# Score products of the first attention: two 128-row passes and four 32-row products side by side, two units at a time

## The chip, the cores and the metric

One core of a Trainium2 chip runs the whole kernel. The metric is the device time of one execution in microseconds. Five engines work side by side, each through its own queue in order: TensorE (PE, with its weight loads PEld), VectorE (DVE), ScalarE (ACT), GpSimd (POOL) and SyncE (SP), which issues the DMAs. They wait for each other through semaphores. TensorE writes to PSUM, here eight banks of 128 x 512 float32. VectorE and ScalarE read it from there.

## The reference

An encoder of two layers over 1024 positions of width 1024. Layer 0 is multi-head latent attention with 16 heads, layer 1 is differential attention. The change lies in layer 0:

```python
sc = (jnp.einsum('bqhd,bkhd->bhqk', qn, k_nope)
      + jnp.einsum('bqhd,bkd->bhqk', qr, k_rope))
p = jax.nn.softmax(sc.astype(jnp.float32), axis=-1)
return jnp.einsum('bhqk,bkhd->bqhd', p.astype(v.dtype), v)
```

`qn` and `k_nope` have 64 elements for each head, `qr` and `k_rope` have 32, and `k_rope` is the same for all heads. Everything is float32.

## The kernel before

Products keep float32's precision by splitting each operand in a high part, rounded to the type fp32r, and a low part, the rest. A product of two operands is then three matmuls: high by high, high by low, low by high.

**Layout.** For each head the keys lie in `Kh` (high) and `Kl` (low), 96 rows by 1024 columns: rows 0 to 63 are `k_nope`, rows 64 to 95 the rotated `k_rope`. The queries of a head and half lie in one page `Q` of 96 rows: `Q[:, 0]` high, `Q[:, 1]` low, 512 columns each. Three buffers of `Kh` and `Kl` go round over the heads; the rope rows of two of them are copied by DMA before the stage. The rope rows of the queries were computed earlier, went to DRAM (`RD`), and come back by two DMAs of 64 KB for each head and half (L820).

**A unit** is one head and one tile of 128 queries; there are 128 units, numbered head by head, eight to a head. `Unit0.scores` makes 128 x 1024 scores by six matmuls of 96 rows and 512 columns (L868 to L870) into a PSUM tile `S` of two banks. `maximum` (L874, DVE) takes the row maximum. `softmax` makes the exponentials with their row sums (L879, ACT), the reciprocal of the sums (L880, DVE) and the scaled page `p` (L881, POOL). Then `transposes` turns `p` into two PSUM tiles `T` by eight 128 x 128 transposes (L845), and `split` takes each `T` out as a high part (ACT, in the helper `hi`, L97) and a low part (DVE, L853). The low part reads `T` and the high part. Two units make a `Chunk`; `pv0` multiplies its 256 columns with the values by 16 matmuls (L905), and `out0` takes the result out: a copy (L913, ACT), an addition (L914, DVE), a product with the gate (L915, POOL).

PSUM holds two `S` tiles, two `T` tiles and two `A` tiles, eight banks in all.

**The order** is written out by hand for all engines: each engine runs its instructions in the order in which the loop emits them. The loop goes over steps `u` from -2 to 129. Step `u` scores unit `u + 2`, finishes the softmax of unit `u + 1`, transposes and splits unit `u`, and on even steps multiplies the chunk of units `u - 2` and `u - 1`:

```python
units[u + 2].scores()                  # PE
units[u + 1].softmax()                 # ACT, DVE, POOL
ps = pv0(ch // 4, chunks[ch])          # even steps: PE
tps = chunks[u // 2].transposes(units[u])
units[u + 2].maximum()                 # DVE
chunks[u // 2].split(units[u], tps)    # ACT, DVE, twice
out0(ch // 4, ch % 4, ps)              # even steps
for fn in fill.get(u, ()): fn()
```

**Fills** are other work put at the end of chosen steps. For each later pair of heads (seven of them, 16 steps each) four odd steps hold a half of the keys or the queries: `k_half` (six matmuls of 512 columns, then two copies on ACT, two subtractions on DVE) and `q_half` (nine matmuls, two copies of 64 x 512 at L822, two subtractions at L825, and the DMAs of the rope rows). Twelve steps hold a part of the values (`v_rows`). Steps 44, 52, ... 100 make a tile of distances for the second layer on DVE (`dist_tile`, L962 and L963), with its absolute value on ACT (L1072) in the step behind. The output projection's weights are split in odd steps from 105 on. The keys and queries of the first two heads are made before the stage, while TensorE works on the gates.

All large tiles come from one pool of 49 pages of 4 KB for each partition.

In the second layer `Unit1.scores` (L1333) multiplies 64-row operands: two matmuls in turn, on rows 0 to 63 and on rows 64 to 127.

Of the kernel before, what the change touches and what calls it, by code (L numbers as in the profile page):

```python
# [21 lines left out]
NPAGES = 49  # L22
# [33 lines left out]
def body(tc, x, c, positions, ada_w, ada_b, norm_g, mla_w_in, mla_q_norm_g, mla_w_q_up,  # L56
# [4 lines left out]
    with ctx:  # L61
# [533 lines left out]
        latH, latL, Kh, Kl, lats = [], [], [], [], {}  # L595
# [39 lines left out]
        def lat_turn(hf):  # L635
# [15 lines left out]
            if hf == 0:  # L651
                Kh.append(page((QK0, D), F32R, "Kh"))
                Kl.append(page((QK0, D), F32R, "Kl"))
            hi("A", Kh[0][NOPE:QK0, sl], tp[0:ROPE, :])
            V.tensor_tensor(Kl[0][NOPE:QK0, sl], tp[0:ROPE, :], f(Kh[0][NOPE:QK0, sl]), op=ALU.subtract)
# [134 lines left out]
        Qt = {}  # L790
# [21 lines left out]
        def q_half(pr, qw, hf, psum=A_):  # L812
# [3 lines left out]
            for i in range(2):  # L816
                h = 2 * pr + i
                q = Qt[h, hf] = page((QK0, 2, 512), F32R, "Q")
                for z in range(2):
                    nc.sync.dma_start(f(q[NOPE:QK0, z]), f(RD[z, h, :, hf * 512:(hf + 1) * 512]))  # L820
                src = ps[i * 64:(i + 1) * 64, :]
                A.activation(q[0:64, 0], src, AF.Copy, scale=SC0)  # L822
            for i in range(2):
                q, src = Qt[2 * pr + i, hf], ps[i * 64:(i + 1) * 64, :]
                V.scalar_tensor_tensor(q[0:64, 1], src, SC0, f(q[0:64, 0]), op0=ALU.mult, op1=ALU.subtract)  # L825

        def k_half(pr, kw, hf, psum=A_):
# [3 lines left out]
            for i in range(2):  # L831
                b = (2 * pr + i) % 3
                src = ps[i * 64:(i + 1) * 64, :]
                hi("A", Kh[b][0:64, sl], src)
            for i in range(2):
                b = (2 * pr + i) % 3
                src = ps[i * 64:(i + 1) * 64, :]
                V.tensor_tensor(Kl[b][0:64, sl], src, f(Kh[b][0:64, sl]), op=ALU.subtract)
# [16 lines left out]
        class Unit0:  # L855
# [4 lines left out]

            def scores(self):
                q = Qt[self.h, self.qt // 4]
                b = self.h % 3
                sl = slice((self.qt % 4) * P, (self.qt % 4 + 1) * P)
                self.ps = S_()
                for n in range(2):
                    kn = slice(n * 512, (n + 1) * 512)
                    T.matmul(self.ps[:, n], q[:, 0, sl], Kh[b][:, kn], start=True, stop=False)  # L868
                    T.matmul(self.ps[:, n], q[:, 0, sl], Kl[b][:, kn], start=False, stop=False)  # L869
                    T.matmul(self.ps[:, n], q[:, 1, sl], Kh[b][:, kn], start=False, stop=True)  # L870
# [5 lines left out]
            def softmax(self):  # L876
                l = cl(1, "l", 4)
                p = self.p = page(name="p")
                A.activation(p.rearrange("p (a b) -> p a b", b=512), self.ps, AF.Exp, bias=self.m, accum_out=l)  # L879
# [735 lines left out]
```

## Time and profile before

| what | value |
|---|---|
| median of three runs | 1628.02 us (1627.78 to 1628.41) |
| the profiled execution | 1632.43 us, of it 1630.7 us from the first to the last instruction |
| busy shares of that span | PE 95%, PEld 81%, DVE 73%, ACT 51%, POOL 28% |
| first score matmul of layer 0 | 246.5 us |
| last score matmuls of layer 0 | from 748.8 us |

Times inside the profile count from its first instruction. A row of the timeline gives start, duration, engine, line, operation, output and inputs, and in brackets how long the engine had been idle and what ended that. Instructions of one kind that follow each other are one row, with their count. The duration of a matmul runs on past the start of the next one, so the pace of TensorE is read from starts, not from durations.

### The profile page before, as it was taken

Reading aid. Unit: us, or ns where it says so; the run is one execution under the profiler, and the core shown is the slowest. Engines: PE = TensorE matmul, PEld = TensorE weight load, DVE = VectorE, ACT = ScalarE, POOL = GpSimd, SP = SyncE. Lnnn points to the kernel's source line nnn. Section 1 sums busy time; section 2 is a strip of 40 time slices with the busy share of each in tenths; the row PEclk is TensorE's granted clock in tenths of the full one; section 3 lists DMA queues with packets and bytes.
Section 4 is the critical chain, followed back from the end, with each engine's and each line's share of the span. In section 5 each row is a group of like instructions: output and inputs, shape, how many; then the busy total and the mean of one; then the engine's idle time right before and its main releaser. Section 6 shows DMA issues by size and latency. Waiting matters only on the chain. (4 is left out here: it accounts for less than half of the span.)

```text
span 1630.7 us, 24823 instructions
## 1 busy us (share of the span) xinstructions
PE 1556.4 (95%) x9231; PEld 1328.9 (81%) x9231; DVE 1183.4 (73%) x2260; ACT 824.1 (51%) x1633; POOL 463.1 (28%) x436
## 2 busy tenths in 40 slices
PE   5999999999999999999999999999999999998897
PEld 4997887888888888888887888788877887776786
DVE  5476877888988888885546667777776677677764
ACT  6343126766777777784123444444543444444511
POOL 1032544444444453572352111111111011110422
PEclk8799999999999999999999999999999999999899
DMA  9007851100110111211233123423232223125122
GB/s 362 30 23 252 259 171 62 45 27 28 53 53 28 65 35 47 96 48 40 103 119 127 65 91 104 130 78 117 78 104 77 92 78 117 52 74 198 46 97 91
DMA packets 91586, 153.32 MB, mean 94 GB/s; under 512 B 5873, under 2 KB 60231, under 8 KB 91465
## 3 DMA queue, kind: packets, MB, share of 16 engines
q1 hardware_dynamic: 91464, 151.73, 28.0%
q8 instruction: 73, 1.20, 0.3%
q14 instruction: 49, 0.39, 0.1%
HBM read 126.01 MB, written 25.17 MB: 93 GB/s over the span
## 5 line engine op out<-in xcount | busy, mean ns | idle before, releaser
L853 DVE TENSOR_TENSOR ptl<-T,pth 128x512 fp32r<-128x512 f32 x384 | 246.3, 683 | 42.2 <-ACT pth L97 42.2
L97 ACT ACTIVATE pth<-T 128x512 fp32r<-128x512 f32 x384 | 207.4, 590 | 92.7 <-PE T L845 87.4
L1339 DVE CUSTOM_DVE_ANT_0 p<-S,dist 128x1024 f32<-128x1024 f32 x128 | 156.1, 1220 | 118.9 <-PE S L1333 111.0
L1347 ACT ACTIVATE p<-p,m 128x1024 f32<-128x1024 f32 x128 | 147.6, 1153 | 172.5 <-DVE m L1341 160.3
L104 POOL TENSOR_TENSOR wbl<-wblk,wbh 128x1024 fp32r<-128x1024 f32 x32 | 77.4, 2423 | 524.9 <-DVE wbh L99 326.9
L845 PE MATMUL T<-ident,p 128*128 128x128 f32 x1536 | 208.0, 278 | 7.0 <-DVE ptl L853 4.0
L845 PEld LDWEIGHTS T<-ident,p 128*128 128x128 f32 x1536 | 172.2, 141 | 44.7 <-issue 13.8
L881 POOL TENSOR_SCALAR p<-p,l 128x1024 f32<-128x1024 f32 x128 | 144.1, 1126 | 152.7 <-DVE l L880 106.7
L1199 PE MATMUL A<-hT,wbh 128*128 128x512 f32 x408 | 164.7, 404 | 1.9 <-DVE KK L1211 1.9
L1200 PE MATMUL A<-hT,wbh 128*128 128x512 f32 x408 | 160.4, 393 | 0.0
L1201 PE MATMUL A<-hT,wbl 128*128 128x512 f32 x408 | 159.9, 392 | 0.0
L874 DVE TENSOR_REDUCE m<-S 128x1 f32<-128x1024 f32 x128 | 155.9, 1218 | 2.3 <-PE S L870 0.3
L879 ACT ACTIVATE p<-S,m 128x1024 f32<-128x1024 f32 x128 | 143.1, 1118 | 14.6 <-DVE m L874 9.8
L868 PE MATMUL S<-Kh,Q 96*128 96x512 f32 x256 | 108.7, 425 | 5.3 <-ACT p L879 3.6
L1333 PE MATMUL S<-KK,QQ 64*128 64x512 f32 x768 | 109.5, 415 | 3.6 <-DVE m L1339 3.6
L869 PE MATMUL S<-Kl,Q 96*128 96x512 f32 x256 | 100.9, 394 | 0.0
L870 PE MATMUL S<-Kh,Q 96*128 96x512 f32 x256 | 100.8, 394 | 0.0
L1199 PEld LDWEIGHTS A<-hT,wbh 128*128 128x128 f32 x408 | 77.3, 189 | 17.6 <-DVE KK L1211 2.4
L1333 PEld LDWEIGHTS S<-KK,QQ 64*128 64x128 f32 x768 | 69.0, 188 | 27.2 <-issue 6.4
L915 POOL TENSOR_TENSOR og<-ot,og 64x256 f32<-64x256 f32 x64 | 54.1, 845 | 130.6 <-DVE ot L914 128.5
L1201 PEld LDWEIGHTS A<-hT,wbl 128*128 128x128 f32 x408 | 77.3, 190 | 16.8
L1200 PEld LDWEIGHTS A<-hT,wbh 128*128 128x128 f32 x408 | 77.5, 190 | 14.7
(342 smaller groups left out, 3508.0 us busy)
## 6 DMA issues: line engine op xcount, KB each, us to landing
dist<-DD SPq DMA_DIRECT2D x64, 512.0 KB, 4.0
adaw<-in_ada_w_dram SPq DMA_DIRECT2D x48, 512.0 KB, 6.6
wblk<-in_diff_w_in_dram SPq DMA_DIRECT2D x32, 512.0 KB, 5.6
qraw<-in_mla_w_q_up_dram SPq DMA_DIRECT2D x16, 288.0 KB
x<-in_x_dram SPq DMA_DIRECT2D x8, 512.0 KB, 5.7
wraw<-in_mla_w_in_dram SPq DMA_DIRECT2D x8, 512.0 KB
OGD<-gt SPq DMA_DIRECT2D x8, 512.0 KB, 6.9
Q<-RD SPq DMA_DIRECT2D x64, 64.0 KB, 2.0
```

Source lines behind the costliest of these rows:

```text
L97: A.activation(o, i, AF.Copy)
L845: T.transpose(tp[:, i * P:(i + 1) * P], p[:, kt * P:(kt + 1) * P], ident)
L853: V.tensor_tensor(ptl[n][:, :, o], src, f(pth[n][:, :, o]), op=ALU.subtract)
L874: V.tensor_reduce(self.m, self.ps, axis=AX.XY, op=ALU.max, negate=True)
L879: A.activation(p.rearrange("p (a b) -> p a b", b=512), self.ps, AF.Exp, bias=self.m, accum_out=l)
L881: G.tensor_scalar(p, p, l, 1.0, op0=ALU.mult, op1=ALU.mult)
L1199: T.matmul(ps, w[0][:, k], a, start=k == 0, stop=False)
L1200: T.matmul(ps, w[0][:, k], b, start=False, stop=False)
L1201: T.matmul(ps, w[1][:, k], a, start=False, stop=k == 7)
L1333: T.matmul(self.ps[c_][:, n], q[r, zq, sl], k[zk][r, n * 512:(n + 1) * 512], start=i == 0, stop=i == 2)
L1339: V.tensor_tensor_reduce(out=p, in0=self.ps[c_].rearrange("p a b -> p (a b)"), in1=dist[self.u], op0=ALU.subtract, op1=ALU.max, scale=1.0, ...
L1347: A.activation(p, p, AF.Exp, bias=self.m[c_], scale=2.0 ** -(self.h + 1), accum_out=L0[self.h][:, self.qt:self.qt + 1] if c_ == 0 else sel ...
```

## The change

The 96 rows of a score product are laid out anew. `KA` has 128 rows: `k_nope` high, rope high, rope low. `KB` has 128 rows: `k_nope` low, then `k_nope` high again. `Q[:, 0]` holds the query's high part, and the rope's high part twice; `Q[:, 1]` the query's high part again and its low part. `KA` by `Q[:, 0]` and `KB` by `Q[:, 1]` then hold all terms but one: rope low (query) by rope high (key). That one has 32 rows. It is done for two units at once by `part`: four matmuls of 32 rows and 512 columns on the four quarters of the rows, from `KC` (the rope keys, laid out in four quarters) and `QC` (the low rope queries of a pair of heads), into the four banks of two `S` tiles. A unit has four score matmuls of 128 rows, and a pair of units four small ones ahead of them.

With that, `k_half` and `q_half` copy each high part twice on ACT (four copies instead of two), and `q_half` issues six DMAs instead of two for each head and half. The pool has 48 pages, since `KC` takes a constant half page.

The loop is written anew. Even steps score units `u + 2` and `u + 3`, take both maxima, and make both exponentials: the first ahead of the split of unit `u`, the second behind it. Both `S` tiles are taken in the same step. The fills of odd steps stand ahead of the transposes and the split of that step, the fills of even steps at the end.

```diff
@@ -19,7 +19,7 @@
 D = 1024
 NT = D // P
 EPS = 1e-6
-NPAGES = 49
+NPAGES = 48
 AHEAD = 2
 
 QR, KVR, ROPE = 384, 256, 32
@@ -592,7 +592,8 @@
             A.activation(r, r, AF.Sin)
             trig.append(r)
         cosA, sinA = trig
-        latH, latL, Kh, Kl, lats = [], [], [], [], {}
+        latH, latL, KA, KB, lats = [], [], [], [], {}
+        KC = cst([P, 512], "KC", F32R)
 
         def latents(st, side=iter(())):
 
@@ -649,10 +650,10 @@
             for j in range(4):
                 T.transpose(tp[0:ROPE, j * P:(j + 1) * P], krs[:, j, :], ident)
             if hf == 0:
-                Kh.append(page((QK0, D), F32R, "Kh"))
-                Kl.append(page((QK0, D), F32R, "Kl"))
-            hi("A", Kh[0][NOPE:QK0, sl], tp[0:ROPE, :])
-            V.tensor_tensor(Kl[0][NOPE:QK0, sl], tp[0:ROPE, :], f(Kh[0][NOPE:QK0, sl]), op=ALU.subtract)
+                KA.append(page((P, D), F32R, "KA"))
+                KB.append(page((P, D), F32R, "KB"))
+            hi("A", KA[0][NOPE:QK0, sl], tp[0:ROPE, :])
+            V.tensor_tensor(KA[0][QK0:P, sl], tp[0:ROPE, :], f(KA[0][NOPE:QK0, sl]), op=ALU.subtract)
             yield 1
 
 
@@ -787,7 +788,7 @@
                 h_, l_ = t[:, 2 * s2:2 * s2 + 2, 0:64], t[:, 2 * s2:2 * s2 + 2, 64:128]
                 V.tensor_tensor(l_, pv[:, :, i], f(h_), op=ALU.subtract)
 
-        Qt = {}
+        Qt, Qc = {}, {}
 
         def qk_load(pr):
             h0 = 2 * pr
@@ -815,14 +816,21 @@
                 lambda k: latH[k][:, hf * 512:(hf + 1) * 512], lambda k: latL[k][:, hf * 512:(hf + 1) * 512])
             for i in range(2):
                 h = 2 * pr + i
-                q = Qt[h, hf] = page((QK0, 2, 512), F32R, "Q")
+                q = Qt[h, hf] = page((P, 2, 512), F32R, "Q")
+                if i == 0 and hf == 0:
+                    Qc[pr] = page((P, 2, 2, 2, P), F32R, "QC")
+                c = Qc[pr][:, i, hf]
+                for r in (NOPE, QK0):
+                    nc.sync.dma_start(f(q[r:r + ROPE, 0]), f(RD[0, h, :, hf * 512:(hf + 1) * 512]))
+                for g in range(4):
+                    nc.sync.dma_start(f(c[g * 32:(g + 1) * 32]), f(RD[1, h, :, hf * 512:(hf + 1) * 512].rearrange(
+                        "p (a j b) -> p a j b", a=2, j=2)[:, :, g // 2]))
+                src = ps[i * 64:(i + 1) * 64, :]
                 for z in range(2):
-                    nc.sync.dma_start(f(q[NOPE:QK0, z]), f(RD[z, h, :, hf * 512:(hf + 1) * 512]))
-                src = ps[i * 64:(i + 1) * 64, :]
-                A.activation(q[0:64, 0], src, AF.Copy, scale=SC0)
+                    A.activation(q[0:64, z], src, AF.Copy, scale=SC0)
             for i in range(2):
                 q, src = Qt[2 * pr + i, hf], ps[i * 64:(i + 1) * 64, :]
-                V.scalar_tensor_tensor(q[0:64, 1], src, SC0, f(q[0:64, 0]), op0=ALU.mult, op1=ALU.subtract)
+                V.scalar_tensor_tensor(q[64:P, 1], src, SC0, f(q[0:64, 0]), op0=ALU.mult, op1=ALU.subtract)
 
         def k_half(pr, kw, hf, psum=A_):
             sl = slice(hf * 512, (hf + 1) * 512)
@@ -831,11 +839,12 @@
             for i in range(2):
                 b = (2 * pr + i) % 3
                 src = ps[i * 64:(i + 1) * 64, :]
-                hi("A", Kh[b][0:64, sl], src)
+                hi("A", KA[b][0:64, sl], src)
+                hi("A", KB[b][64:P, sl], src)
             for i in range(2):
                 b = (2 * pr + i) % 3
                 src = ps[i * 64:(i + 1) * 64, :]
-                V.tensor_tensor(Kl[b][0:64, sl], src, f(Kh[b][0:64, sl]), op=ALU.subtract)
+                V.tensor_tensor(KB[b][0:64, sl], src, f(KA[b][0:64, sl]), op=ALU.subtract)
 
         def transpose_unit(p, pth, ptl, j, n):
 
@@ -858,27 +867,32 @@
             def __init__(self, u):
                 self.h, self.qt = divmod(u, 8)
 
+            def part(self):
+
+                c, pr = Qc[self.h // 2][:, self.h % 2, self.qt // 4], self.qt % 4 // 2
+                for g in range(4):
+                    r = slice(g * 32, (g + 1) * 32)
+                    T.matmul(units[8 * self.h + self.qt + g // 2].ps[:, g % 2], c[r, pr], KC[r, :], start=True, stop=False)
+
             def scores(self):
-                q = Qt[self.h, self.qt // 4]
-                b = self.h % 3
+                q, b = Qt[self.h, self.qt // 4], self.h % 3
                 sl = slice((self.qt % 4) * P, (self.qt % 4 + 1) * P)
-                self.ps = S_()
-                for n in range(2):
-                    kn = slice(n * 512, (n + 1) * 512)
-                    T.matmul(self.ps[:, n], q[:, 0, sl], Kh[b][:, kn], start=True, stop=False)
-                    T.matmul(self.ps[:, n], q[:, 0, sl], Kl[b][:, kn], start=False, stop=False)
-                    T.matmul(self.ps[:, n], q[:, 1, sl], Kh[b][:, kn], start=False, stop=True)
+                for z, k in enumerate((KA, KB)):
+                    for n in range(2):
+                        T.matmul(self.ps[:, n], q[:, z, sl], k[b][:, n * 512:(n + 1) * 512], start=False, stop=z == 1)
 
             def maximum(self):
                 self.m = cl(1, "m", 4)
                 V.tensor_reduce(self.m, self.ps, axis=AX.XY, op=ALU.max, negate=True)
 
-            def softmax(self):
-                l = cl(1, "l", 4)
-                p = self.p = page(name="p")
-                A.activation(p.rearrange("p (a b) -> p a b", b=512), self.ps, AF.Exp, bias=self.m, accum_out=l)
-                V.reciprocal(l, l)
-                G.tensor_scalar(p, p, l, 1.0, op0=ALU.mult, op1=ALU.mult)
+            def exp(self):
+                self.l = cl(1, "l", 4)
+                self.p = page(name="p")
+                A.activation(self.p.rearrange("p (a b) -> p a b", b=512), self.ps, AF.Exp, bias=self.m, accum_out=self.l)
+
+            def norm(self):
+                V.reciprocal(self.l, self.l)
+                G.tensor_scalar(self.p, self.p, self.l, 1.0, op0=ALU.mult, op1=ALU.mult)
 
         class Chunk:
 
@@ -1040,10 +1054,11 @@
                 vw, qkw = v_load(0), qk_load(0)
             if m == 6:
                 for i in (1, 2):
-                    Kh.append(page((QK0, D), F32R, "Kh"))
-                    Kl.append(page((QK0, D), F32R, "Kl"))
-                    nc.sync.dma_start(f(Kh[i][NOPE:QK0, :]), f(Kh[0][NOPE:QK0, :]))
-                    nc.sync.dma_start(f(Kl[i][NOPE:QK0, :]), f(Kl[0][NOPE:QK0, :]))
+                    KA.append(page((P, D), F32R, "KA"))
+                    KB.append(page((P, D), F32R, "KB"))
+                    nc.sync.dma_start(f(KA[i][NOPE:P, :]), f(KA[0][NOPE:P, :]))
+                for g in range(4):
+                    nc.sync.dma_start(f(KC[g * 32:(g + 1) * 32, :]), f(KA[0][NOPE:QK0, (g % 2) * 512:(g % 2 + 1) * 512]))
                 for hf in range(2):
                     k_half(0, kw, hf, T_)
                 for hf in range(2):
@@ -1083,31 +1098,47 @@
         part = []
         with tc.manual_schedule(engines=MAN):
             for u in range(-2, NU + 2):
-                if u + 2 < NU:
-                    units[u + 2].scores()
-                if 0 <= u + 1 < NU:
-                    units[u + 1].softmax()
+                even, cur = u % 2 == 0, 0 <= u < NU
+                nxs = units[u + 2:u + 4] if even else []
+                for nx in nxs:
+                    nx.ps = S_()
+                if nxs:
+                    nxs[0].part()
+                for nx in nxs:
+                    nx.scores()
+                if not even:
+                    for fn in fill.get(u, ()):
+                        fn()
+                if cur:
+                    tps = chunks[u // 2].transposes(units[u])
                 if u in (NU - 2, NU):
                     part.append(S_())
                 if u in (NU - 2, NU - 1):
                     for k in (range(4) if u < NU - 1 else range(4, 7)):
                         out_k(part[0], 0, oT, wo, k)
-                done = u % 2 == 0 and u >= 2
+                done = even and u >= 2
                 if done:
                     ch = u // 2 - 1
                     ps = pv0(ch // 4, chunks[ch])
                 if u == NU:
                     out_mm(part[1], 1, oT, wo, range(7))
-                if 0 <= u < NU:
-                    tps = chunks[u // 2].transposes(units[u])
-                if u + 2 < NU:
-                    units[u + 2].maximum()
-                if 0 <= u < NU:
+                for nx in nxs:
+                    nx.maximum()
+                for nx in nxs[:1]:
+                    nx.exp()
+                if not even and u + 2 < NU:
+                    units[u + 2].norm()
+                if cur:
                     chunks[u // 2].split(units[u], tps)
+                for nx in nxs[1:]:
+                    nx.exp()
+                for nx in nxs[:1]:
+                    nx.norm()
                 if done:
                     out0(ch // 4, ch % 4, ps)
-                for fn in fill.get(u, ()):
-                    fn()
+                if even:
+                    for fn in fill.get(u, ()):
+                        fn()
 
 
         A1, B1 = ab1
```

## Prediction

> **What bounds the kernel now.** I read the page first, then the sums over the stretch of layer 0's attention, then the timeline of plain steps engine by engine.
>
> ```profile
> span 1630.7 us, 24823 instructions
> ## 1 busy us (share of the span) xinstructions
> PE 1556.4 (95%) x9231; PEld 1328.9 (81%) x9231; DVE 1183.4 (73%) x2260; ACT 824.1 (51%) x1633; POOL 463.1 (28%) x436
> ```
> ```profile
> 246.40:754.00 507.60, 492.09 (x3160) 433.03 (x3159) 429.51 (x723) 372.83 (x706) 239.22 (x237) 1.00 0.15 49
> ```
>
> The second fence is one row of the windows view: stretch, length, then busy time of PE, PEld, DVE, ACT and POOL, then the granted clock, the DMA share and GB/s. The stage takes 507.6 us for 128 units. PE is busy for 492.1 us of it, DVE for 429.5, ACT for 372.8. So TensorE bounds the stage, and the others run beside it with 78 and 135 us to spare. That spare time counts only if the order of the queues lets it be used.
>
> The timeline of a stretch without fills shows the order on VectorE and ScalarE and the pace of each step:
>
> ```profile
> 743.97 1.23 DVE L874 TENSOR_REDUCE m<-S 128x1 f32<-128x1024 f32 x1
> 745.11 1.28 DVE L853 TENSOR_TENSOR ptl<-T,pth 128x512 fp32r<-128x512 f32 x2
> 746.53 0.16 DVE L880 RECIPROCAL l<-l 128x1 f32<-128x1 f32 x1
> 746.61 1.23 DVE L874 TENSOR_REDUCE m<-S 128x1 f32<-128x1024 f32 x1
> 748.53 1.29 DVE L853 TENSOR_TENSOR ptl<-T,pth 128x512 fp32r<-128x512 f32 x2 [0.70 <-ACT pth L97]
> 749.85 0.43 DVE L914 TENSOR_TENSOR ot<-A,ot 64x256 f32<-64x256 f32 x1
> 750.65 0.16 DVE L880 RECIPROCAL l<-l 128x1 f32<-128x1 f32 x1 [0.37 <-ACT p L879]
> 750.84 1.23 DVE L874 TENSOR_REDUCE m<-S 128x1 f32<-128x1024 f32 x1
> ```
> ```profile
> 745.29 1.12 ACT L879 ACTIVATE p<-S,m 128x1024 f32<-128x1024 f32 x1 [0.57 <-DVE m L874]
> 746.30 0.19 ACT L879 ACTIVATION_READ_ACCUMULATOR p<-S,m 128x1 f32 x1
> 747.90 1.09 ACT L97 ACTIVATE pth<-T 128x512 fp32r<-128x512 f32 x2 [1.41 <-PE T L845]
> 749.01 0.38 ACT L913 ACTIVATE ot<-A 64x256 f32<-64x256 f32 x1
> 749.41 1.12 ACT L879 ACTIVATE p<-S,m 128x1024 f32<-128x1024 f32 x1
> 750.42 0.19 ACT L879 ACTIVATION_READ_ACCUMULATOR p<-S,m 128x1 f32 x1
> 750.52 1.08 ACT L97 ACTIVATE pth<-T 128x512 fp32r<-128x512 f32 x2
> ```
> ```profile
> 746.24 1.12 PE L905 MATMUL A<-ptl,V 128*128 128x256 f32 x8
> 747.21 1.03 PE L845 MATMUL T<-ident,p 128*128 128x128 f32 x8
> 748.00 0.47 PE L868 MATMUL S<-Kh,Q 96*128 96x512 f32 x1
> ```
>
> A plain pair of units takes 6.87 us (two maxima apart: 743.97 to 750.84). The exponential at 749.41 did not wait for a maximum: that one had ended at 747.84, a whole unit's work earlier. This distance of one step between a maximum and its exponential is what lets ACT and DVE work at the same time.
>
> **TensorE's part.** Twelve 96-row matmuls a pair become eight of 128 rows and four of 32 rows side by side. That side-by-side products really overlap is shown by layer 1, where 64-row products go two by two:
>
> ```profile
> 877.05 0.40 PE L1201 MATMUL A<-hT,wbl 128*128 128x512 f32 x1
> 877.29 0.39 PE L1199 MATMUL A<-hT,wbh 128*128 128x512 f32 x1
> 877.52 0.39 PE L1200 MATMUL A<-hT,wbh 128*128 128x512 f32 x1
> 877.74 0.39 PE L1201 MATMUL A<-hT,wbl 128*128 128x512 f32 x1
> 878.06 1.66 PE L1333 MATMUL S<-KK,QQ 64*128 64x512 f32 x12
> 879.65 0.50 PE L1199 MATMUL A<-hT,wbh 128*128 128x512 f32 x1
> 879.99 0.40 PE L1200 MATMUL A<-hT,wbh 128*128 128x512 f32 x1
> ```
>
> From 877.74 to 879.99 there are eight slots: one full product, six pairs of half-row products, one full product. Consecutive full products stand 0.23 us apart (877.05 to 877.74, three slots). Eight such slots are 1.84 us; they took 2.25. Going into and out of the split array therefore costs up to 0.41 us; with a single slot inside, the gap from 877.74 to 878.06 (0.09 over a slot) and the two from the way out (0.32 and 0.34, together 0.20 over) give about 0.29. A pair of units loses three slots, 0.69 us, and pays 0.29 to 0.41: a gain of 0.28 to 0.40, over 64 pairs 18 to 26 us. That is the most that TensorE can give. A plain pair would need about 5.95 us of it: 9 x 0.23 + 0.36 for the scores, two times 0.79 for transposes (747.21 to 748.00) and two times 0.97 for the values (746.24 to 747.21).
>
> **The order's part.** The new loop emits for an even step e: both maxima, exponential of e + 2, split of e, exponential of e + 3, copy of `out0`; then, in the odd step, fills, and the split of e + 1. The next pair's first exponential follows directly behind that split on ACT, but it needs its own maximum, which stands on DVE behind the low part of that same split. So a ring closes that the old order did not have. With the start of the first maximum as 0:
>
> - maximum 1.23, and 0.09 to the exponential (743.97 + 1.23, then 745.29): exponential at 1.32
> - exponential to first high copy 1.11 (749.41 to 750.52), high copies of e at 2.43
> - two high copies 1.11 (747.90 to 749.01): second exponential at 3.54
> - then 1.11: copy of `out0` at 4.65, and 0.40 (749.01 to 749.41): high copies of e + 1 at 5.05
> - first high copy to first low part 0.63 (747.90 to 748.53): 5.68
> - two low parts and on to DVE's next operation, 1.32 at most (748.53 to 749.85), 1.2 if back to back: next maximum at 6.9 to 7.0
>
> I take 6.95. TensorE fits inside: transposes of e + 1 wait for the `T` tiles until about 4.4, the scores run from 4.85 and the first unit's end at about 6.6, ahead of 6.95 by 0.35. POOL's norms lie between 4.4 and 7.5, a step ahead of their transposes. So a plain pair costs 0.08 us more than before: the gain of TensorE is gone, and of each ring ACT waits 6.95 - (4 x 1.11 + 0.40) = 2.11 us, from the last high copy to the next exponential.
>
> **The fills' part.** In a ring that ACT and DVE set, whatever a fill puts on ACT lengthens the ring, since it stands between `out0`'s copy and the split of e + 1. Before, it ran beside TensorE. The new copies are 56 (28 each for keys and queries in the stretch):
>
> ```profile
> L97 ACT ACTIVATE Kh<-A 64x512 fp32r<-64x512 f32 x28 | 16.7, 595 | 5.6 <-PE A L133 5.4
> L822 ACT ACTIVATE Q<-A 64x512 fp32r<-64x512 f32 x28 | 16.6, 594 | 17.5 <-PE A L133 17.2
> L97 ACT ACTIVATE V<-A 128x128 fp32r<-128x128 f32 x48 | 9.4, 282 | 6.1 <-PE A L133 6.1
> ```
> ```profile
> L963 DVE SCALAR_TENSOR_TENSOR dist<-kpl,posT,dist 128x1024 f32<-128x1024 f32 x8 | 13.2, 1646 | 0.3
> ...
> L104 DVE TENSOR_TENSOR oT<-og,oT 128x512 fp32r<-128x512 f32 x8 | 7.0, 906 | 0.0
> L962 DVE TENSOR_SCALAR dist<-kph,posT 128x1024 f32<-128x1024 f32 x8 | 6.0, 744 | 0.1
> ```
>
> 56 x 0.60 = 33.6 us. Eight distance tiles stand on DVE behind `out0`'s addition (at 5.1, done 5.5): 0.74 + 1.65 more, so ACT gets its absolute value at about 7.95 instead of 5.05. With nothing else it waits 2.9 us (two of them), with the four copies of a value fill ahead (9.4 / 48 each, 0.8) 2.1 (two), with a query fill 0.5 (four): 12 us. Ten query fills without a distance tile make ACT wait for TensorE's nine matmuls, 0.3 each: 3 us. For the smaller DVE fills that ACT now waits for (the low parts of `oT` alone are 7.0 us) I allow 10.
>
> **The sum, by ACT's time in the stage.** Its work 372.8, new copies 33.6, ring waits 62 x 2.11 = 131 (63 rings, the first two without all parts), distance 12, query 3, small fills 10: 562.4. Before it was 507.6. That is 54.8 us more.
>
> **What it costs beside that.** The six instead of two DMAs for each head and half: eight issues took 5.18 us before the stage, so 24 take 15.5, from 226.6 to about 242, and the stage begins at 246.4; two more for the key copies fit in too. Later halves have two steps of time and more for twelve issues (7.8 us). Cost nothing; without that cover, some microseconds once.
>
> ```profile
> 226.60 5.18 SPq L820 DMA_DIRECT2D Q<-RD  x8
> ```
>
> One page fewer in the pool and more pages in use (`QC`, one more `p`) can make a split wait for a page. Nothing in this trace prices it. From below: 0. From above: each high copy of e would wait for the values' product that reads the recycled pages, until about 3.07 instead of 2.43, 0.64 us x 62 = 40. I take 0 and let the range reach half of it.
>
> **The clock.** Waiting TensorE can lose its clock. Here is where that happened in this stage:
>
> ```profile
> 732.10:735.50 3.40, 1.73 (x13) 1.18 (x11) 3.40 (x7) 3.05 (x7) 1.22 (x2) 1.00 0.02 5
> 735.50:738.90 3.40, 3.40 (x12) 2.83 (x11) 3.40 (x7) 2.51 (x5) 2.72 (x2) 0.50 0.00 0
> ```
> After 3.40 us in which PE was busy for 1.73, the clock (the third number from the end) was 0.50 for the next 3.40. In a ring with a distance tile TensorE would stand idle for some 3.1 us (scores done at 7.2, `T` free at 10.3). Eight such rings at up to 1.7 us each are 0 to 14 us; most of it is hidden behind the ring's slack, and I take 4. The Trainium skill's page "TensorE: Matmul & The Clock Gate", section "Part 1: The HAM clock gate", asks for a whole idle window of about 3.4 us before the clock halves; by it a pause of 3.1 would cost 0. The trace does not agree: a stretch that was half idle was enough here, so the 4 stay.
>
> Together 1632.4 + 54.8 + 4 = 1691.2 for the profiled execution. The median before lies 4.4 below its profiled execution (1628.0 against 1632.4), so 1687.
>
> **The rivals.**
>
> A. *TensorE stays the bound.* If DVE and ACT keep up, 64 pairs save 18 to 26 us: 1602 to 1610. For it speak the busy sums: 492 against 430 and 373. Against it speaks the ring, which holds whatever the sums are. It decides if the ring closes in less than the 6.5 us that TensorE would then take for a pair (6.87 less 0.40), 0.45 below what I add up. Chance 0.05. The Trainium skill's page "TensorEngine Tiling (Array Packing)", section "Performance Considerations", warns that a faster array shifts the limit to emptying PSUM. Taken as throughput that warning would not bite here, as 430 us of DVE fit in the 492 - 26 left to TensorE, and rival A would follow; what bites is the order.
>
> B. *Fills stay hidden.* If ACT could do the new copies in the 2.1 us of waiting, only 62 x 0.08 = 5 us and the distance tiles remain: about 1628 + 5 + 5 = 1638. Against it: the fills stand ahead of the split, the wait behind it. 0.04.
>
> C. *The four small products go one after another.* Then the pair's scores end 0.69 us later, 7.3 instead of 6.6, 0.35 past the ring: 62 x 0.35 = 22, so 1709. Layer 1's pairs speak against it. 0.04.
>
> D. *Pages or clock cost their upper bounds*: 40 for the pages, 10 more for the clock, 1697 to 1737, about 1725. 0.10.
>
> **How the numbers follow.** The forecast has 0.77, 1687 us, by itself 1665 to 1705, as the ring may be 0.1 shorter (6 us) and the allowances 10 too large, or 10 too small with the clock at its upper bound. For 8 in 10 I reach from 1655 to 1715. A difference of about 0.2%, 3 us, is what a measurement of this kernel can tell from none. Faster by more than that: rival A, 0.05. Within it: 0.02, where A's gain and the ring would cancel. Slower: 0.93.
>
> **What would show it.** If right: in the stage's stretch PE's busy share falls well below its 97%, the clock no longer stays at 1.00, a plain pair has its first maxima 6.9 to 7.0 us apart, ACT's first exponential of each pair waits about 2 us for `m`, and rings with a key or query fill last 9.3 us. The four small products start within a few ns of each other. Layer 1 and everything ahead of 246 us keep their times. Wrong if first maxima stand 6.5 us apart in plain pairs, if the first exponential of a pair does not wait, or if layer 1 grew.

## The result, and the profile after

| | before | after |
|---|---|---|
| median of three runs | 1628.02 us | 1712.89 us (1710.15 to 1713.44) |
| the profiled execution | 1632.43 us | 1713.44 us |
| first maximum of the stage's first pair | 248.35 us | 247.80 us |
| first maximum of its last pair | 746.61 us | 829.15 us |

The ratio is 1.0521, with a 95% interval of 1.0501 to 1.0541: slower, by 85 us. Between the profiled executions it is 81.0 us, of which the stage of layer 0's attention takes 83.1 (581.35 against 498.26 between the maxima in the table). The work ahead of it and behind it lost nothing. The head of the page:

```profile
span 1711.7 us, 25156 instructions
## 1 busy us (share of the span) xinstructions
PE 1554.8 (91%) x9231; PEld 1299.4 (76%) x9231; DVE 1184.4 (69%) x2260; ACT 851.4 (50%) x1697; POOL 465.7 (27%) x436
```

TensorE executes as many instructions as before, for nearly the same busy time. The stage in the windows view, with the columns of the prediction's second fence:

```profile
246.40:838.00 591.60, 492.52 (x3156) 405.09 (x3153) 433.31 (x733) 396.76 (x764) 242.43 (x238) 0.97 0.16 50
```

PE is busy for 83% of the stage, down from 97%. DVE is at 73% and ACT at 67%: no engine is full. What fills the time shows in the waits of the stage (who waits for whom, us in total, times, longest):

```profile
ACT p L891 <- DVE m L886: 129.8, 52, 4.1
...
PE T L854 <- DVE ptl L862: 89.6, 56, 4.0
...
DVE KB L847 <- ACT KB L97: 26.9, 13, 2.7
```

In the stage before, the first of these was

```profile
ACT p L879 <- DVE m L874: 9.8, 14, 2.1
```

So the exponential's wait for its maximum went from 9.8 us to 129.8, and TensorE waits 89.6 us (4.0 before) for the low parts that free the `T` tiles. A plain ring, from one pair's first maximum to the next pair's, on ACT, DVE and PE:

```profile
422.12 1.11 ACT L891 ACTIVATE p<-S,m 128x1024 f32<-128x1024 f32 x1 [2.06 <-DVE m L886]
...
423.23 1.08 ACT L97 ACTIVATE pth<-T 128x512 fp32r<-128x512 f32 x2
424.18 1.12 ACT L891 ACTIVATE p<-S,m 128x1024 f32<-128x1024 f32 x1
...
425.43 0.38 ACT L927 ACTIVATE ot<-A 64x256 f32<-64x256 f32 x1
425.83 1.09 ACT L97 ACTIVATE pth<-T 128x512 fp32r<-128x512 f32 x2
428.98 1.12 ACT L891 ACTIVATE p<-S,m 128x1024 f32<-128x1024 f32 x1 [2.06 <-DVE m L886]
```
```profile
420.82 2.34 DVE L886 TENSOR_REDUCE m<-S 128x1 f32<-128x1024 f32 x2
423.85 1.29 DVE L862 TENSOR_TENSOR ptl<-T,pth 128x512 fp32r<-128x512 f32 x2 [0.69 <-ACT pth L97]
...
426.46 1.29 DVE L862 TENSOR_TENSOR ptl<-T,pth 128x512 fp32r<-128x512 f32 x2
427.67 2.35 DVE L886 TENSOR_REDUCE m<-S 128x1 f32<-128x1024 f32 x2
```
```profile
424.69 1.16 PE L854 MATMUL T<-ident,p 128*128 128x128 f32 x8 [0.42 <-DVE ptl L862]
425.78 0.51 PE L875 MATMUL S<-KC,QC 32*128 32x512 f32 x4
...
428.18 1.03 PE L854 MATMUL T<-ident,p 128*128 128x128 f32 x8
```

First maxima stand 6.85 us apart (420.82 to 427.67). The scores of the new pair begin at 425.78 and are done before 428.18, and the maximum starts in between, directly behind the low parts on DVE: it does not wait for TensorE. ACT then waits 2.06 us for it. The four 32-row products show in one row: they start within 10 ns of each other.

The same views one ring later, with a fill of the keys:

```profile
432.28 0.38 ACT L927 ACTIVATE ot<-A 64x256 f32<-64x256 f32 x1
432.69 0.59 ACT L97 ACTIVATE KA<-A 64x512 fp32r<-64x512 f32 x1
...
434.50 0.59 ACT L97 ACTIVATE KB<-A 64x512 fp32r<-64x512 f32 x1
435.12 1.08 ACT L97 ACTIVATE pth<-T 128x512 fp32r<-128x512 f32 x2
439.13 1.12 ACT L891 ACTIVATE p<-S,m 128x1024 f32<-128x1024 f32 x1 [2.93 <-DVE m L886]
```
```profile
435.12 1.39 DVE L847 TENSOR_TENSOR KB<-A,KA 64x512 fp32r<-64x512 f32 x2 [1.94 <-ACT KB L97]
...
436.62 1.29 DVE L862 TENSOR_TENSOR ptl<-T,pth 128x512 fp32r<-128x512 f32 x2
437.82 2.35 DVE L886 TENSOR_REDUCE m<-S 128x1 f32<-128x1024 f32 x2
```

The ring lasts 10.15 us (427.67 to 437.82). From `out0`'s copy to the high parts ACT needs 2.84 instead of the plain ring's 0.40: four copies, 2.44. The two subtractions start 0.03 us after the fourth copy has ended (434.50 + 0.59), though the first needs only the first copy's result. So they hold DVE, and the low parts start 1.50 after the first high copy (435.12 to 436.62) instead of 0.63: 0.87 more. 6.85 + 2.44 + 0.87 = 10.16.

The kinds of rings side by side (us between first maxima):

| ring | before | forecast | after |
|---|---|---|---|
| plain (11) | 5.7 to 7.3, mean 6.68 | 6.95 | 6.85 to 6.95 |
| with a value fill (10) | 6.6 to 7.9, mean 7.46 | 7.75 | 7.87 to 7.89, one 8.24 |
| with a key or query fill (24) | 7.4 to 9.0, three 10.3 to 11.4 | 9.35 | 10.0 to 10.2, nine 10.4 to 12.8 |
| with a distance tile (8) | 8.5 to 9.8 | 10.9 | 10.7 to 10.9 |

The forecasts for value fills and distance tiles are worked out from the prediction's own figures: 6.95 and the four copies' 0.8; 6.95, the 2.9 us of waiting and the absolute value itself, 1.06 (8.5 us for eight in the stage).

Of the stage's 83.1 us, 48.9 lie in the 24 rings with a key or query fill, 12.3 in the eight with a distance tile, 8.4 in the six that split output weights and gated values, 6.4 in the first four, 4.6 in the ten with a value fill, and only 2.5 in the eleven plain ones. The ring costs little by itself; it costs where fills, which ran beside TensorE before, now lengthen it.

### The profile page after: what moved, and what is told of

It is laid out like the page before. It is cut to its first block, busy times and chain, and to the rows that moved or that the text cites. A ratio compares the mean times of both kernels' runs of the same rounds, so it can differ in the third digit from the quotient of the medians.

```text
span 1711.7 us, 25156 instructions
## 1 busy us (share of the span) xinstructions
PE 1554.8 (91%) x9231; PEld 1299.4 (76%) x9231; DVE 1184.4 (69%) x2260; ACT 851.4 (50%) x1697; POOL 465.7 (27%) x436
## 5 line engine op out<-in xcount | busy, mean ns | idle before, releaser
L854 PE MATMUL T<-ident,p 128*128 128x128 f32 x1536 | 220.4, 286 | 93.1 <-DVE ptl L862 89.6
L891 ACT ACTIVATE p<-S,m 128x1024 f32<-128x1024 f32 x128 | 143.6, 1122 | 162.4 <-DVE m L886 129.8
L886 DVE TENSOR_REDUCE m<-S 128x1 f32<-128x1024 f32 x128 | 150.2, 1213 | 6.8 <-PE S L882 6.8
L350 PE MATMUL S<-woh,oT 128*128 128x512 f32 x224 | 88.7, 396 | 0.0
L882 PE MATMUL S<-KA,Q 128*128 128x512 f32 x256 | 87.7, 424 | 0.0
L352 PE MATMUL S<-woh,oT 128*128 128x512 f32 x224 | 87.3, 390 | 0.0
L351 PE MATMUL S<-wol,oT 128*128 128x512 f32 x224 | 87.3, 390 | 0.0
```

Source lines behind the costliest of these rows:

```text
L854: T.transpose(tp[:, i * P:(i + 1) * P], p[:, kt * P:(kt + 1) * P], ident)
L886: V.tensor_reduce(self.m, self.ps, axis=AX.XY, op=ALU.max, negate=True)
L891: A.activation(self.p.rearrange("p (a b) -> p a b", b=512), self.ps, AF.Exp, bias=self.m, accum_out=self.l)
```

## The experiments

My theory was the ring of the prediction: the order costs the time through ACT and DVE, and each ACT copy of a fill in front of the second split lengthens it. Its rival was the layout: its products, their way into and out of the split array, or the place of its copies cost the time whatever the order. The first two kernels cut the change in two.

**order_alone**: the new loop with the old layout (`Kh`, `Kl`, 96 rows).

```diff
-                if nxs:
-                    nxs[0].part()
...
-                hi("A", KA[b][0:64, sl], src)
-                hi("A", KB[b][64:P, sl], src)
+                hi("A", Kh[b][0:64, sl], src)
```

> The old 96-row layout (six score matmuls a unit, two copies for a half of keys or queries, no small products) in the new order (units in pairs, both S tiles at once). Ring theory: the order alone makes the loss. Plain pairs stay at 6.85 us, as in the changed kernel; rings with a key or query fill lose two of four ScalarE copies, 10.15 - 2 x 0.605 = 8.9; 24 of them make 1713 - 29 = 1684 us (1676 to 1692). Layout theory (the new operands, their copies and DMAs make the loss): about 1628 us, plain pairs 6.5 to 6.9 and no 2 us wait of ScalarE.

Measured: 1684.42 us, ratio 1.0343 (1.0323 to 1.0362). Plain rings stay at 6.85, key rings come to 8.94 us, distance rings stay at 10.9. The order alone costs 56 us, with not one product changed, and 28.5 of the 85 us need the layout as well. What a key ring adds can be read on DVE:

```profile
429.95 1.39 DVE L838 TENSOR_TENSOR Kl<-A,Kh 64x512 fp32r<-64x512 f32 x2 [0.74 <-ACT Kh L97]
...
431.44 1.29 DVE L853 TENSOR_TENSOR ptl<-T,pth 128x512 fp32r<-128x512 f32 x2
```

The high parts start at 429.94 on ACT, so the low parts follow after 1.50 here too, 0.87 more than in a plain ring; two copies add 1.23: 6.85 + 1.23 + 0.87 = 8.95. The 0.87 comes with the order, whatever the layout. What the layout adds to such a ring is the time of two more copies.

**layout_alone**: the new layout in the old order; each unit makes its own two 32-row products ahead of its four large ones.

```diff
-                for g in range(4):
+                for n in range(2):
+                    g = 2 * (self.qt % 2) + n
                     r = slice(g * 32, (g + 1) * 32)
-                    T.matmul(units[8 * self.h + self.qt + g // 2].ps[:, g % 2], c[r, pr], KC[r, :], start=True, stop=False)
+                    T.matmul(self.ps[:, n], c[r, pr], KC[r, :], start=True, stop=False)
```

> The new 128-row layout with its copies, DMAs and 48 pages in the old order, one unit at a time; each unit has its own two 32-row products side by side ahead of its four passes. Ring theory: TensorE bounds again; a unit has five slots of 0.23 us and 0.29 to 0.41 for going in and out of the split array against six slots before, so 0.06 to 0.18 more for each of 128 units: 1636 to 1651 us, and the doubled copies of ScalarE stay hidden. Layout theory: near the changed kernel's 1713 us, above 1690.

Measured: 1655.8 us, ratio 1.016 (1.0145 to 1.0175), a few microseconds over the upper end. PE is busy for 96% of the stage (512.46 us of 531.60, from 246.4 to 778.0): in rings with a fill it is still the bound, and it got slower. A ring with a key fill on PE, first of the kernel before, then of this one:

```profile
478.60 1.04 PE L845 MATMUL T<-ident,p 128*128 128x128 f32 x8
479.39 0.48 PE L868 MATMUL S<-Kh,Q 96*128 96x512 f32 x1
...
480.86 1.07 PE L845 MATMUL T<-ident,p 128*128 128x128 f32 x8
481.68 0.48 PE L131 MATMUL A<-latH,kw 128*128 128x512 f32 x1
...
483.14 0.40 PE L868 MATMUL S<-Kh,Q 96*128 96x512 f32 x1
...
484.52 1.12 PE L905 MATMUL A<-pth,V 128*128 128x256 f32 x8
...
486.44 0.82 PE L845 MATMUL T<-ident,p 128*128 128x128 f32 x6
```
```profile
492.51 1.04 PE L854 MATMUL T<-ident,p 128*128 128x128 f32 x8
493.47 0.50 PE L876 MATMUL S<-KC,QC 32*128 32x512 f32 x2
...
495.15 1.16 PE L854 MATMUL T<-ident,p 128*128 128x128 f32 x8
496.07 0.48 PE L131 MATMUL A<-latH,kw 128*128 128x512 f32 x1
...
497.62 0.50 PE L876 MATMUL S<-KC,QC 32*128 32x512 f32 x2
...
499.08 1.10 PE L926 MATMUL A<-pth,V 128*128 128x256 f32 x8
...
500.99 1.04 PE L854 MATMUL T<-ident,p 128*128 128x128 f32 x8
```

From transposes to transposes it takes 8.48 us instead of 7.84. Transposes to scores take 0.96 instead of 0.79; the scores themselves, up to the values, 1.46 instead of 1.38, though they have five slots instead of six; the way from the fill's products 0.09 more; 0.21 more passes before the second transposes, and 0.10 from these to the fill's products. The saved slot is less than the way in and out, when each unit pays it. Key and query rings hold 22.0 of the 26.7 us by which the stage grew between the first maxima of its first and last pair; plain rings did not grow (mean 6.57 us against 6.68), so there the way in and out stays hidden. The pair by pair `part` of the real change pays it once for two units, and that needs both `S` tiles at once, hence the new order.

**copies_from_sbuf**: the second copies are made from the first ones, behind the subtractions on ACT's and DVE's lists.

```diff
                 hi("A", KA[b][0:64, sl], src)
-                hi("A", KB[b][64:P, sl], src)
...
+            for i in range(2):
+                b = (2 * pr + i) % 3
+                hi("A", KB[b][64:P, sl], f(KA[b][0:64, sl]))
```

> The changed kernel with the second copy of each high part made from the first one in SBUF, behind the subtractions, instead of from PSUM ahead of them; as many ScalarE copies as before. Theory for the part of the loss that was not forecast: a subtraction that reads a PSUM tile waits for the last copy emitted ahead of it that reads the same tile, so four copies in a row hold it back. Then the first subtraction starts behind the second copy, rings with a key or query fill go from 10.15 to about 9.3 us, 24 x 0.85 = 20 us: 1692 us (1686 to 1700). If the 10.15 us come from the number of copies alone: 1713 us.

Measured: 1695.85 us, ratio 1.0406 (1.0391 to 1.0422). Most rings with key and query fills take 9.1 to 9.3 us instead of 10.0 to 10.2. ACT makes the same number of copies, and 17 us are gone: the subtractions now run beside the second copies, and the low parts start 0.63 after the first high copy again (436.10 on ACT, 436.73 on DVE). This part of the loss was what the subtractions, held until the last copy from the PSUM tile, put in front of the low parts.

**copies_on_gpsimd**: as copies_from_sbuf, with the second copies on GpSimd.

```diff
-                hi("A", KB[b][64:P, sl], f(KA[b][0:64, sl]))
+                hi("G", KB[b][64:P, sl], f(KA[b][0:64, sl]))
```

> The changed kernel with its 56 second copies made by GpSimd, from the first copy in SBUF, so that ScalarE and the subtractions see the old number of copies; GpSimd is busy 243 us of this stage's 592 and one such copy should take about 0.8 us there (by the row of 128x256 fp32r<-128x256 f32 at 408 ns for half the columns). If ScalarE's time and the wait for its last copy are what the second copies cost, the rings with key and query fills come to 8.9-9.0 as with the old layout in the new order, and the kernel takes 1683-1687 us: the products saved on TensorE are then worth nothing and the copies 28 us. If the cost is the place in SBUF or the new layout's own products, the rings stay over 9.2 and it takes 1695 or more.

Measured: 1686.09 us, ratio 1.0356 (1.0334 to 1.0379). Most rings with key and query fills take 8.94 to 9.1 us, plain ones 6.85. That is the old layout's time in the new order, to within the intervals. So the copies on ACT are the whole price of the layout in this order, as far as the intervals tell, and what it saves on TensorE is worth nothing there.

**copy_in_the_wait**: `out0`'s copy moves behind the second split into ACT's wait, its addition behind the next maxima.

```diff
                 if done:
-                    out0(ch // 4, ch % 4, ps)
+                    o0 = out0(ch // 4, ch % 4, ps)
+                if not even:
+                    next(o0, 0)
```

> The changed kernel with one move: the copy of out0 on ScalarE stands behind the split of the odd unit, where ScalarE waits, and its addition on VectorE behind the next two maxima. Nothing is added or left out. Ring theory: each ring is shorter by that copy's slot of 0.40 us, plain pairs 6.45, 62 x 0.40 = 25 us in all: 1688 us (1680 to 1694). If instead TensorE or the taking of both S tiles at once sets the pace, a move on ScalarE changes nothing: 1713 us.

Measured: 1684.3 us, ratio 1.0328 (1.0311 to 1.0346), 4 us less than expected. Plain rings go to 6.63 us and not to 6.45: the first maximum now waits 0.18 us for the scores of its unit (at 414.94, released by PE L882). The prediction had these scores done at about 6.6, and that is the limit which the shortened ring meets. Other rings gained more, most key rings 0.57 (to 9.58) and rings with a distance tile about 0.6 to 0.9; most query rings gained nothing (10.1 to 10.3). Moving one 0.4 us copy and its addition gives 28 us, 23.5 of them between the stage's first and last maxima, with every product of the layout in place: the order of ACT's list sets the time.

**fills_in_the_wait** goes further: the fills' matmuls stay where they are, their copies follow the second split, their subtractions the next maxima. The other fills of odd steps (absolute values of distances, weights to split) move behind the second split whole. **fills_in_the_wait_old_layout** is the same with the old layout.

```diff
+                gens = [fn() for fn in fill3.get(u, ())]
+                for g in gens:
+                    next(g)
...
+                if not even:
+                    later = [outs] + gens
+                    for g in later:
+                        next(g, 0)
```

> The changed kernel with all its work, and the fills of keys, queries and values taken apart: their matmuls ahead of the odd unit's transposes, their ScalarE copies and out0's copy behind the odd unit's split, where ScalarE waits, their subtractions and out0's addition behind the next pair's two maxima. Ring theory: the wait of 2 us takes up the copies, so a ring is set by TensorE and the T tiles: plain 6.63 as with out0's copy alone, key rings 7.3 to 7.5, query rings 8.0, value rings 7.4 to 7.6, distance rings 8 to 10; 23 x 6.63 + 14 x 7.4 + 14 x 8.0 + 12 x 7.5 and some 35 for distances and the rest make 493 us from the first to the last pair, where the kernel before takes 498: about 1623 us (1608 to 1635). If the paired tiles or the layout cost by themselves, beyond the ring: above 1650 us.

> The same order with the old layout: six 96-row matmuls a unit, two copies for a half of keys or queries, no small products. In this order TensorE is close to the bound, so the layout's gain on TensorE (0.2 to 0.4 us a pair, 13 to 26 us in all) should show as a difference to fills_in_the_wait: 1636 to 1645 us. If the layout's gain is lost to ScalarE's extra copies or to the way in and out of the split array even here: no slower than fills_in_the_wait.

Measured: 1660.34 us, ratio 1.0206 (1.0188 to 1.0223), and 1658.94 us, ratio 1.0191 (1.0172 to 1.021) with the old layout. Both were missed, though the first is 53 us under the changed kernel. Plain rings take 6.64 and the first key ring after them 7.53, as worked out. Fills that follow each other take 8.8 (keys) and 9.5 (queries). The waits of fills_in_the_wait and a row of its PE show why:

```profile
PEld A L930 <- DVE ot L940: 52.4, 40, 1.9
```
```profile
433.24 1.21 PE L930 MATMUL A<-pth,V 128*128 128x256 f32 x8 [0.98 <-DVE ot L940]
```

The product with the values waits for an `A` tile, since `out0`'s addition, which frees it, now stands behind two maxima. A wait taken from ACT came back on TensorE, through a buffer. That the two layouts take the same time is a balance. On DVE a plain ring's first maximum, with the new layout and then with the old:

```profile
414.20 2.36 DVE L897 TENSOR_REDUCE m<-S 128x1 f32<-128x1024 f32 x2 [0.18 <-PE S L893]
```
```profile
410.72 2.59 DVE L884 TENSOR_REDUCE m<-S 128x1 f32<-128x1024 f32 x2
```

With the new layout it waits for the scores, with the old one it does not: plain rings take 6.64 and 6.47 us. Key rings go the other way, 7.53 and 8.77 with the new layout, 7.82 and 8.85 with the old.

**addition_early** puts that addition back ahead of the maxima, and **addition_early_old_layout** is the same with the old layout.

```diff
+                next(outs, 0)
                 for nx in nxs:
                     nx.maximum()
```

> The kernel of fills_in_the_wait with one step moved back: out0's addition stands on VectorE ahead of the next pair's maxima, and only the subtractions of the fill stay behind them, so that the tile A is free for the next value product a maximum earlier. If the wait of the value product for A (0.98 us in the quoted ring) was what held the rings with fills, key rings come to 7.5-7.6 us, query rings to about 8.4, value rings to 7.6, plain ones stay at 6.6, and the kernel takes about 1617 us (1605 to 1635), at or under the kernel before. If the rings with fills are held by ACT's or VectorE's sum of work, it stays at 1650-1662.

> The same order with the old 96-row layout (three products for each half, nothing side by side). If TensorE sets the pace of the plain rings in this order, the layout's gain of about 0.2 us a pair shows and this one is some 10-15 us slower than addition_early; if the ring of ScalarE and VectorE still sets it, the layout's second copies cost as much as its products save and the two lie within 6 us of each other.

Measured: 1654.71 us, ratio 1.0178 (1.0154 to 1.0201), and 1650.15 us, ratio 1.015 (1.0128 to 1.0171) with the old layout, within the 6 us of the second case. The wait for `A` went, and rings with one key fill take 7.6 us, as worked out; the total was missed, since plain rings went from 6.64 to 7.18. The edit did more than I had written: its line runs in odd steps too, and there it puts `out0`'s copy back ahead of the second split. So the ring is the changed kernel's 6.85 with the addition's 0.33 on DVE.

**addition_early_copy_late** mends that: the line runs in even steps alone, the copy stays behind the second split. **addition_early_copy_late_old_layout** is the same with the old layout.

```diff
-                next(outs, 0)
+                if even:
+                    next(outs, 0)
```

> addition_early with out0's copy left behind the second split on ScalarE, where fills_in_the_wait has it (addition_early had put it back ahead of the split, which its plain rings of 7.18 us show: 6.85 + the addition's 0.33 on VectorE). The addition alone stays ahead of the next maxima. Now the plain ring should be 6.64 + 0.33 = 6.95 to 7.0 if only its place on VectorE counts; or, since the addition needs the copy and the copy starts 1.1 us after the second split began, the addition holds the maxima until the copy is done and the plain ring stays at about 7.2. About 30 plain rings and rings with values hang on it: 1646-1650 us in the first case, 1653-1658 in the second. It is over the kernel before in both.

> The same with the old 96-row layout. addition_early_old_layout was 4.6 us under addition_early; with the copy out of the first part of ScalarE's ring the second copies of the layout still lie in ScalarE's wait, so I expect this one equal to the new layout within 5 us, 1644-1656.

Measured: 1645.47 us, ratio 1.0099 (1.0083 to 1.0116), and 1641.43 us, ratio 1.0081 (1.0064 to 1.0099) with the old layout, the one just under its first range, the other under its range but within 5 us of the first. The plain ring is 6.70 with either layout, shorter than both of my figures. On ACT and DVE its links can be read off one by one:

```profile
404.64 1.12 ACT L902 ACTIVATE p<-S,m 128x1024 f32<-128x1024 f32 x1 [1.93 <-DVE m L897]
...
405.75 1.08 ACT L97 ACTIVATE pth<-T 128x512 fp32r<-128x512 f32 x2
406.70 1.13 ACT L902 ACTIVATE p<-S,m 128x1024 f32<-128x1024 f32 x1
...
407.87 1.14 ACT L97 ACTIVATE pth<-T 128x512 fp32r<-128x512 f32 x2
```
```profile
403.34 2.34 DVE L897 TENSOR_REDUCE m<-S 128x1 f32<-128x1024 f32 x2
...
408.50 1.29 DVE L873 TENSOR_TENSOR ptl<-T,pth 128x512 fp32r<-128x512 f32 x2 [0.39 <-ACT pth L97]
409.71 0.41 DVE L940 TENSOR_TENSOR ot<-A,ot 64x256 f32<-64x256 f32 x1
410.04 2.34 DVE L897 TENSOR_REDUCE m<-S 128x1 f32<-128x1024 f32 x2
```

From maximum to exponential 1.30, to the high parts 1.11, to the second exponential 0.95, to the second high parts 1.17, to their low parts 0.63, to the addition 1.21, to the next maximum 0.33: 6.70. Without the addition these links would give 6.37, so the 6.64 of fills_in_the_wait was not this ring's but the wait for the scores, and adding 0.33 to it was wrong. This is the best of the new orders with the new layout, 67 us under the changed kernel with the same products.

**fills_in_the_wait_gpsimd**: fills_in_the_wait with the second copies on GpSimd.

> The order of fills_in_the_wait (1660) with the second copies on GpSimd. There the wait of the value product for the tile A set the rings with fills, with either layout, so it should take 1655-1660 us, no less; if ScalarE's second copies were still on the path, it falls to 1635-1645.

Measured: 1660.15 us, ratio 1.0201 (1.0182 to 1.0221), the same as with the copies on ACT. There the second copies on ACT are no longer on the path.

None of these kernels beats the one before. In each of the three mended orders that ran with both layouts, the old one took as long or less: 1658.94 against 1660.34, 1650.15 against 1654.71, 1641.43 against 1645.47. The intervals overlap each time; in the second pair the runs themselves do not (1649.31 to 1652.38 against 1653.44 to 1658.78). A gain of the new layout is in none of the three.

## Why the prediction was right, point by point

The forecast was 1687 us, 1665 to 1705 by itself. The 1712.89 us lie above that and just inside the range of 1655 to 1715. The mechanism was the one that was named; that the range still holds the time is in part luck, since it was left wide for pages, clock and allowances, and most of the excess came from a term that it did not price.

**The ring of the order.** Right. Plain rings take 6.85 to 6.95 against 6.95; the exponential waits 2.06 us against 2.11; TensorE finishes the scores before the maximum's turn. order_alone shows it without the layout, and copy_in_the_wait by moving one copy.

**TensorE's part.** Nearly right, and without weight. From the first small product to the next transposes it takes 2.40 us (425.78 to 428.18), against 9 x 0.23 + 0.36 = 2.43. What I left out is the way in: the transposes ahead of the scores take 1.09 to the first small product (424.69 to 425.78), of which some is their own wait; without it, in layout_alone's rows, 0.96 against 0.79. So the gain is nearer 0.2 us a pair than the 0.28 to 0.40 of the prediction. copies_on_gpsimd shows that it buys nothing in this order.

**The fills' part: the term that was mis-sized.** The prediction put 56 x 0.60 us on ACT, 9.35 us for a ring with a key or query fill. In 15 of the 24 it was 10.0 to 10.2, in nine more. The step "whatever a fill puts on ACT lengthens the ring" held, but the fill also lies on DVE: its subtractions start when the last copy of the same PSUM tile has ended, and the low parts of the second split stand behind them (0.87 in the rows of this kernel and of order_alone). Against the forecast that is 0.8 us in each of 24 rings (28 fills, four of them with a distance tile that hides it), 19 us of the 22 by which the profiled execution exceeds the forecast (81.0 against 58.8). The nine longer ones of these rings add some 10 us more; for waits like theirs the prediction had terms of their own (query fills, small fills, clock). copies_from_sbuf got 17 us back. The trace of before had it already: the two subtractions of a query fill begin just behind the second copy (362.82 and 1.21 for two), not behind the first, though DVE stood idle for 1.83 us by then:

```profile
362.82 1.21 ACT L822 ACTIVATE Q<-A 64x512 fp32r<-64x512 f32 x2 [1.48 <-PE A L133]
```
```profile
364.06 1.41 DVE L825 SCALAR_TENSOR_TENSOR Q<-A,Q 64x512 fp32r<-64x512 f32 x2 [1.83 <-ACT Q L822]
```

**The DMAs, the pages.** Taken at nothing, and rightly: the stage starts at the same time as before, and no wait for a page or a `Q` transfer stands among the stage's large waits.

**The clock.** Its mean in the stage fell from 1.00 to 0.97, so it did not stay full, as the prediction said. In the stage it was at 0.50 in ten stretches of 3.4 us, against one before: from 649.20 to 652.60, for example, PE was busy for 0.70 us, and the next 3.40 us had 0.50. Six of the nine longer key and query rings hold such a stretch or stand right behind one; they take 10.4 to 11.3 us, 4.1 in all over 10.15 each, where the prediction took 4. order_alone has four such key rings, at 9.4 to 9.6 against 8.94. That goes by their place alone; no run separates it. The other three were long before the change too (10.3 to 11.4).

**The rivals.** A falls: TensorE is not the bound, and no plain ring is 6.5 us long. B falls: fills lengthen the ring by more than their time. C falls by the four starts within 10 ns. Of D, 1725 us, nothing is needed; the time lies near it for another reason.

**Where the gain of TensorE went.** Off the path: the order needed for pairs made ACT and DVE wait for each other, and the layout put copies into exactly that chain.

## What to carry to other kernels

Before an order is changed so that an engine gets fuller batches, walk one period through the lists of the other engines and look for a ring: an operation that waits for a result queued behind something that itself waits for the first engine. Busy shares of 73% to 97% said that everything fitted; the distance of one step between a maximum and its exponential was what made it fit, and the change spent it. When work is added to such a ring, count it on every engine that touches the same buffer, and when work is moved out of it, ask which buffer now comes free later.

## What the runs showed that I had not expected

- A reader of a PSUM tile on DVE started 0.03 us after the last of four ACT reads of that tile (434.50 + 0.59 to 435.12), though its own operand had been ready for 1.8 us (432.69 + 0.59). With the second pair of reads issued behind it (copies_from_sbuf) the ring was 0.9 us shorter. With that pair made on GpSimd (copies_on_gpsimd) it was 1.2 shorter, which is the time of two copies on ACT; the subtractions still started behind the last read that was left. Whether the chip or the way in which waits are put into the program orders them by the last one stays open.
- Going from the 128-row transposes to 32-row products cost 0.17 us more than going to 96-row ones (493.47 - 492.51 against 479.39 - 478.60), and a unit with two small and four full products took no less time than one with six (1.46 against 1.38 up to the values).
